# Squared norms of q by a product with a column of ones, in place of transposes with squares along the rows (Gated DeltaNet and Mamba-2 trunk, one core)

## The chip, the core and the metric

The program runs on one core of a Trainium2 chip. A core has a matrix engine (TensorE; PE in the profile, and PEld for its weight loads), a vector engine (VectorE, DVE), an activation engine (ScalarE, ACT), a general engine (GpSimd, POOL) and SyncE (SP), which here issues nearly all transfers. Each engine runs its own list of instructions in order and waits on semaphores for the others. Matrix products and transposes write to PSUM, everything else lies in SBUF or in device memory. The metric is device microseconds of one execution; lower is better.

## What is computed

Two layers over a sequence of 1024 tokens, all in float32. The first is a gated DeltaNet with 8 query/key heads and 16 value heads of width 128; the second, not touched here, is a Mamba-2 mixer. Cut to what matters:

```python
proj = hid @ w_in
qkv = silu(causal_conv(qkv, conv_w))           # 4 taps, per channel
q = _l2norm(q) * 128 ** -0.5                   # _l2norm(x) = x * rsqrt(sum(x*x, -1) + 1e-6)
k = _l2norm(k)
o = _chunk_gated_delta_rule(q, k, v, g, beta)
o = _rmsnorm(o, norm_w) * silu(z)
x = x + o @ w_out
```

The sum of squares of q runs over the 128 channels of a head, one number for each token and head.

## The kernel before

q, k and v are computed transposed: a tile such as `qT` has the 128 channels of a head on the partitions and 512 tokens along the rows, so there are two tiles (`th` 0 and 1) to a head. The normalisation of q is not applied to q itself. The output of a head goes through an RMS norm anyway, so a factor per token can be moved there: `cq` holds, for each token, the epsilon of that norm multiplied by the sum of squares of the token's q. It is read on GpSimd by `so` (L676), just ahead of the power of -0.5 (L678).

The first layer runs over 8 groups (one q/k head and two value heads each). For each group:

- `q_halves`, two `v_halves` and `k_halves` project 512 tokens at a time. One half is 24 products of 128x512 in `ps_proj` (L165 to L167: weights and activations are split into a high and a low part, three products for each of 8 input blocks). ACT copies the result to `raw` (L197) and scales it to `acc` (L200), DVE adds three taps (L204), ACT takes a tanh `th` (L184) and DVE multiplies (L185); for q that gives `qT`.
- What has to be done with a finished half, for q the function `stats`, is put on a list `later` and issued behind the products of the next half, so that TensorE does not stand at it.
- `k_products` squares k for the triangular system and fills `nte` (L437, L441, L451), with decays `lt` from ACT (L418).
- `inverse` inverts the triangular blocks. It stores parts of `nte` to device memory (`xd`, L470), loads them back in another layout (`X`, L473), sets a diagonal on GpSimd (L474), and then runs 31 pairs of DVE instructions, `tm` (L485) and `Dt` (L487).
- `scan` walks over 8 chunks of 128 tokens with a state `S`: a product of k with S (L626), `vpp` on DVE (L629), a product with the inverse (L634), `p` on ACT (L637), a product for the new state (L643), `S` on DVE (L646, L649). Beside it run the output (L661, L663, `o`, `yn`) and the gate `z` (products L227 to L229). `store` transposes `yn` (L66) into `ps_tr`.

The work of neighbouring groups overlaps, and its order on each engine is made by the compiler's list scheduler, which takes instructions by priority and by the readiness that its own model of time gives. A small edit in one function can therefore move instructions of others. Only the order of DVE in the preparation of the first group is written by hand.

`ps_pt` is a ring of two PSUM banks, shared by `stats`, the transposes of v, `k_products` and `inverse`. The tag `th` is a ring of two SBUF tiles, so far for the tanh alone.

In the profile a float32 product appears as two records of weight load and matmul each, a transpose or a product of the split operands as one.

Of the kernel before, what the change touches and what calls it, by code (L numbers as in the profile page):

```python
# [8 lines left out]
F32 = mybir.dt.float32  # L9
F32R = mybir.dt.float32r  # L10
AF = mybir.ActivationFunctionType
ALU = mybir.AluOpType
# [3 lines left out]
EPS = 1e-6  # L16
P = 128
# [7 lines left out]
def hybrid_trunk(  # L25
# [6 lines left out]
    nc = tc.nc  # L32
    x, out = x[0], out[0]
# [6 lines left out]
    cv = ctx.enter_context(tc.tile_pool(name="cv", bufs=2))  # L40
# [12 lines left out]
    ident = const.tile([P, P], F32, tag="ident", name="ident")  # L53
    make_identity(nc, ident)
    ones = const.tile([P, P], F32, tag="ones", name="ones")
# [9 lines left out]
    def turn_pe(dst, src, eye):  # L65
        nc.tensor.transpose(dst, src, eye)  # L66
# [115 lines left out]
    def silu2(dst, src):  # L182
        th = cv.tile([P, 512], F32, tag="th", name="th")
        nc.scalar.activation(th, src, AF.Tanh, scale=0.5)  # L184
        nc.vector.scalar_tensor_tensor(out=dst, in0=th, scalar=1.0, in1=src, op0=ALU.add, op1=ALU.mult)  # L185

    def conv_halves(w_in, col0, hid, cw, ti, bias, emit):
        raws = []

        def consume(th, pt):  # L190
            raw = cv.tile([P, 515], F32, tag="raw", name="raw", bufs=3)
            raws.append(raw)
            if th == 0:
                nc.gpsimd.memset(raw[:, 0:3], 0.0)
            else:
                nc.gpsimd.tensor_copy(raw[:, 0:3], raws[0][:, 512:515])
            nc.scalar.copy(raw[:, 3:515], pt)  # L197
            acc = cv.tile([P, 512], F32, tag="acc", name="acc", bufs=3)
            if bias is None:
                nc.scalar.activation(acc, pt, AF.Copy, scale=cw[:, 96 + ti:97 + ti])  # L200
            else:
                nc.scalar.activation(acc, pt, AF.Identity, scale=cw[:, 96 + ti:97 + ti], bias=bias)  # L202
            for k in range(3):
                nc.vector.scalar_tensor_tensor(out=acc, in0=raw[:, k:k + 512],  # L204
                                               scalar=cw[:, k * 32 + ti:k * 32 + ti + 1], in1=acc,
                                               op0=ALU.mult, op1=ALU.add)
            emit(th, acc)

        yield from proj_halves(w_in, col0, hid, consume)
# [193 lines left out]
    with tc.tile_pool(name="gw", bufs=2) as gw:  # L403
# [140 lines left out]
        def q_halves(g):  # L544
            qT = GS[g]["qT"] = [gw.tile([P, 512], F32, tag="qT", name="qT", bufs=3) for _ in range(2)]
            cq = GS[g]["cq"] = st.tile([P, NT], F32, tag="cq", name="cq")

            def emit(th, acc):
                silu2(qT[th], acc)
                later.append(lambda: stats(th))  # L550

            def stats(th):
                pt = ps_pt()
                for j in range(4):
                    turn_pe(pt[:, j * P:(j + 1) * P], qT[th][:, j * P:(j + 1) * P], ident)
                for j in range(4):
                    nc.scalar.activation(pt[:, j * P:(j + 1) * P], pt[:, j * P:(j + 1) * P], AF.Square,
                                         accum_out=cq[:, th * 4 + j:th * 4 + j + 1])
                if th == 1:
                    nc.gpsimd.tensor_scalar(out=cq, in0=cq, scalar1=4.0 * EPS, scalar2=EPS * P,  # L560
                                            op0=ALU.add, op1=ALU.mult)

            yield from conv_halves(gw_in, g * P, hid, cw_gdn, g, None, emit)

# [429 lines left out]
```

## Time and profile before

| | |
|---|---|
| median of 3 runs | 1995.43 us (1994.64 to 2000.03) |
| the profiled execution | 1990.66 us, its span 1989.0 us |
| TensorE busy | 1919.1 us (96% of the span), weight loads 1639.7 us (82%) |
| VectorE, ScalarE, GpSimd busy | 1305.7 us (66%), 1063.4 us (53%), 411.6 us (21%) |

The span is the time from the first to the last instruction; 1.7 us of the profiled execution lie outside it. The first layer's groups run from about 100 us to about 900 us. A busy TensorE is not one at its peak: its matmuls are pipelined, so records overlap, and the time that a product costs is read from start to start.

### The profile page before, as it was taken

Reading aid. Unit: us, or ns where it says so; the run is one execution under the profiler, and the core shown is the slowest. Engines: PE = TensorE matmul, PEld = TensorE weight load, DVE = VectorE, ACT = ScalarE, POOL = GpSimd, SP = SyncE. Lnnn points to the kernel's source line nnn. Section 1 sums busy time; section 2 is a strip of 40 time slices with the busy share of each in tenths; the row PEclk is TensorE's granted clock in tenths of the full one; section 3 lists DMA queues with packets and bytes.
Section 4 is the critical chain, followed back from the end, with each engine's and each line's share of the span. In section 5 each row is a group of like instructions: output and inputs, shape, how many; then the busy total and the mean of one; then the engine's idle time right before and its main releaser. Section 6 shows DMA issues by size and latency. Waiting matters only on the chain.

```text
span 1989.0 us, 36043 instructions
## 1 busy us (share of the span) xinstructions
PE 1919.1 (96%) x12974; PEld 1639.7 (82%) x12974; DVE 1305.7 (66%) x2915; ACT 1063.4 (53%) x2893; POOL 411.6 (21%) x818
## 2 busy tenths in 40 slices
PE   7997999999999999999999999999999999999998
PEld 5786888888888888897778788888888888888886
DVE  6797685778677776844354676657666676767333
ACT  5635656575656666564343554544555555555332
POOL 1101211212122212100000032423333243332000
PEclk9997999999999999999999999999999999999999
DMA  4421323232232323235574232222222223236654
GB/s 141 117 54 49 98 56 84 67 78 75 57 93 52 99 49 105 58 94 157 152 221 133 64 91 80 69 84 80 64 80 57 80 75 83 78 104 195 203 170 142
DMA packets 284789, 193.35 MB, mean 97 GB/s; under 512 B 65425, under 2 KB 246338, under 8 KB 284610
## 3 DMA queue, kind: packets, MB, share of 16 engines
q1 hardware_dynamic: 284610, 191.05, 34.2%
q8 instruction: 102, 1.67, 0.4%
q14 instruction: 77, 0.63, 0.1%
HBM read 159.34 MB, written 31.65 MB: 96 GB/s over the span
## 4 chain that ended last, share of the span: by engine, by line
PE 75%; DMA 9%; DVE 7%; ACT 4%; POOL 2%; issue 2%; SPq 1%; POOLq 0%; DVEq 0%; ACTq 0%
PE ps_proj L165 9%; PE ps_proj L166 9%; PE ps_proj L167 9%; PE ps_proj L347 6%; PE ps_proj L349 6%; PE ps_proj L348 5%; PE ps_proj L227 5%; PE ps_proj L228 4%; PE ps_proj L229 4%; DMA gcrow<-gcr_s 2%; PE ps_tr L66 2%; PE ps_pt L66 2%; DMA X<-xd 2%; DVE acc L204 2%; PE ps_sc L895 1%
## 5 line engine op out<-in xcount | busy, mean ns | idle before, releaser
L165 PE MATMUL ps_proj<-hid_h,wh 128*128 128x512 f32 x1024 | 412.9, 403 | 3.4 <-ACT acc L200 3.2
L167 PE MATMUL ps_proj<-hid_h,wl 128*128 128x512 f32 x1024 | 404.9, 395 | 0.0
L166 PE MATMUL ps_proj<-hid_l,wh 128*128 128x512 f32 x1024 | 403.6, 394 | 0.0
L227 PE MATMUL ps_proj<-zh,hid_h 128*128 128x256 f32 x1024 | 300.5, 293 | 1.0 <-DVE z L234 1.0
L229 PE MATMUL ps_proj<-zh,hid_l 128*128 128x256 f32 x1024 | 295.4, 288 | 0.0
L228 PE MATMUL ps_proj<-zl,hid_h 128*128 128x256 f32 x1024 | 295.4, 288 | 0.0
L165 PEld LDWEIGHTS ps_proj<-hid_h,wh 128*128 128x128 f32 x1024 | 192.7, 188 | 43.9 <-ACT acc L200 4.0
L167 PEld LDWEIGHTS ps_proj<-hid_h,wl 128*128 128x128 f32 x1024 | 192.5, 188 | 40.3
L166 PEld LDWEIGHTS ps_proj<-hid_l,wh 128*128 128x128 f32 x1024 | 192.9, 188 | 35.4
L347 PE MATMUL ps_proj<-woh,yh 128*128 128x512 f32 x512 | 205.2, 402 | 4.6 <-ACT yh L86 3.2
L348 PE MATMUL ps_proj<-wol,yh 128*128 128x512 f32 x512 | 204.4, 400 | 0.8 <-DVE wol L87 0.7
L349 PE MATMUL ps_proj<-woh,yl 128*128 128x512 f32 x512 | 203.1, 399 | 0.8 <-DVE yl L87 0.7
L227 PEld LDWEIGHTS ps_proj<-zh,hid_h 128*128 128x128 f32 x1024 | 196.3, 192 | 6.0 <-DVE z L234 2.3
L228 PEld LDWEIGHTS ps_proj<-zl,hid_h 128*128 128x128 f32 x1024 | 196.4, 192 | 3.0
L229 PEld LDWEIGHTS ps_proj<-zh,hid_l 128*128 128x128 f32 x1024 | 196.4, 192 | 0.3
L204 DVE SCALAR_TENSOR_TENSOR acc<-raw,cw_ssd,acc 128x512 f32<-128x512 f32 x192 | 156.5, 815 | 45.2 <-ACT acc L202 42.5
L86 ACT CAST yh<-yr 128x512 fp32r<-128x512 f32 x128 | 79.1, 619 | 142.2 <-PE ps_proj L348 90.8
L87 DVE TENSOR_TENSOR yl<-yr,yh 128x512 fp32r<-128x512 f32 x128 | 89.0, 696 | 98.7 <-ACT yh L86 98.3
L204 DVE SCALAR_TENSOR_TENSOR acc<-raw,cw_gdn,acc 128x512 f32<-128x512 f32 x192 | 145.9, 761 | 11.8 <-ACT acc L200 10.2
L87 DVE TENSOR_TENSOR wl<-wr,wh 128x512 fp32r<-128x512 f32 x128 | 89.3, 698 | 68.3 <-ACT wh L86 67.7
L317 POOL TENSOR_SCALAR_AFFINE_SELECT gcrow<-gcrow 128x512 f32<-128x512 f32 x128 | 92.1, 722 | 197.1 <-DMA gcrow<-gcr_g 141.8
L676 POOL TENSOR_SCALAR so<-so,cq 128x2 f32<-128x2 f32 x64 | 27.3, 426 | 462.7 <-ACT yn L675 462.7
(240 smaller groups left out, 3872.0 us busy)
## 6 DMA issues: line engine op xcount, KB each, us to landing
wr<-in_gdn_w_in_dram SPq DMA_DIRECT2D x96, 256.0 KB, 3.0
wr<-in_ssd_w_in_dram SPq DMA_DIRECT2D x96, 256.0 KB, 2.9
gcrow<-gcr_g SPq DMA_DIRECT2D x64, 256.0 KB, 3.6
yr<-y0d SPq DMA_DIRECT2D x64, 256.0 KB, 3.4
gcrow<-gcr_s SPq DMA_DIRECT2D x64, 256.0 KB, 3.9
yr<-y1d SPq DMA_DIRECT2D x64, 256.0 KB, 3.2
y0d<-yg SPq DMA_DIRECT2D x64, 128.0 KB, 1.9
wr<-in_gdn_w_out_dram SPq DMA_DIRECT2D x32, 256.0 KB, 3.5
```

The lines of the kernel that those rows point to most:

```text
L87: nc.vector.tensor_tensor(out=lo, in0=src, in1=hi.bitcast(F32), op=ALU.subtract)
L165: nc.tensor.matmul(pt[0:nco], hi[:, j, 0:nco], xh[:, j, :], start=first, stop=False)
L166: nc.tensor.matmul(pt[0:nco], hi[:, j, 0:nco], xl[:, j, :], start=False, stop=False)
L167: nc.tensor.matmul(pt[0:nco], lo[:, j, 0:nco], xh[:, j, :], start=False, stop=last)
L204: nc.vector.scalar_tensor_tensor(out=acc, in0=raw[:, k:k + 512], scalar=cw[:, k * 32 + ti:k * 32 + ti + 1], in1=acc, op0=ALU.mult, op1=ALU ...
L227: nc.tensor.matmul(pt, xh, zh[:, k, :], start=k == 0, stop=False)
L228: nc.tensor.matmul(pt, xh, zl[:, k, :], start=False, stop=False)
L229: nc.tensor.matmul(pt, xl, zh[:, k, :], start=False, stop=k == KT - 1)
L317: nc.gpsimd.affine_select(out=t, in_=t, pattern=[[0, 4], [1, P]], compare_op=ALU.is_ge, fill=-1e30, base=0, channel_multiplier=-1)
L347: nc.tensor.matmul(pt, yh[:, j, :], hi[:, j, :], start=first, stop=False)
L348: nc.tensor.matmul(pt, yh[:, j, :], lo[:, j, :], start=False, stop=False)
L349: nc.tensor.matmul(pt, yl[:, j, :], hi[:, j, :], start=False, stop=last)
```

## The change

For each of the 16 halves of q, four transposes into PSUM and four squares along the rows (ACT, each with its accumulator read) are replaced by one square of the whole 128x512 tile on ACT into an SBUF tile of the ring `th`, and four products of a squared 128x128 block, as the stationary operand, with one column of ones. The sums then lie in four columns of a PSUM tile. The scaling with epsilon moves from GpSimd, once a group for 8 columns, to DVE, once a half for 4 columns, and reads PSUM.

```diff
             def stats(th):
+                sq = cv.tile([P, 512], F32, tag="th", name="sq")
+                nc.scalar.activation(sq, qT[th], AF.Square)
                 pt = ps_pt()
                 for j in range(4):
-                    turn_pe(pt[:, j * P:(j + 1) * P], qT[th][:, j * P:(j + 1) * P], ident)
-                for j in range(4):
-                    nc.scalar.activation(pt[:, j * P:(j + 1) * P], pt[:, j * P:(j + 1) * P], AF.Square,
-                                         accum_out=cq[:, th * 4 + j:th * 4 + j + 1])
-                if th == 1:
-                    nc.gpsimd.tensor_scalar(out=cq, in0=cq, scalar1=4.0 * EPS, scalar2=EPS * P,
-                                            op0=ALU.add, op1=ALU.mult)
+                    nc.tensor.matmul(pt[:, j:j + 1], sq[:, j * P:(j + 1) * P], ones[:, 0:1], start=True, stop=True)
+                nc.vector.tensor_scalar(out=cq[:, th * 4:th * 4 + 4], in0=pt[:, 0:4], scalar1=4.0 * EPS,
+                                        scalar2=EPS * P, op0=ALU.add, op1=ALU.mult)
```

Lines behind the edit have numbers smaller by 2 in the changed kernel: L626 becomes L624, L634 becomes L632, L646 and L649 become L644 and L647.

The scheduler puts the new instructions where its model has them ready, and the order of the rest of the first layer moves with them; in the second layer the order is that of before. Two places in a group matter to the prediction, and one of them is shown on two engines.

**The second half of q, on TensorE**, in a group where the first scan steps are under way (402 us in the profile of before). Before, the last scan product is followed by the transposes of `qT`:

```order
L643 MATMUL ps_sc<-p,ktok 128x128 x2
L661 MATMUL ps_sc<-S,qT 128x256
L663 MATMUL ps_sc<-p,att 128x128 x2
L626 MATMUL ps_sc<-S,kT 128x256
L66 MATMUL ps_pt<-ident,qT 128x128 x4
L66 MATMUL ps_pt<-ident,acc 128x128 x4
L165 MATMUL ps_proj<-hid_h_96,wh 128x512
```

Now the same place of the changed kernel:

```order
L641 MATMUL ps_sc<-p,ktok 128x128 x2
L659 MATMUL ps_sc<-S,qT 128x256
L661 MATMUL ps_sc<-p,att 128x128 x2
L624 MATMUL ps_sc<-S,kT 128x256
L557 MATMUL ps_pt<-ones,sq 128x1 x4
L632 MATMUL ps_sc<-vpp,nte 128x128 x2
L165 MATMUL ps_proj<-hid_h_96,wh 128x512
```

The new products stand where the transposes stood, directly behind the product of k with S, and now need the square `sq` from ACT where the transposes needed `qT` from DVE. The transposes of `acc` (of v) have moved further back.

**The same place on ACT.** Before, `L670` (the output's scaling) is followed by the eviction `L200`, and the squares read PSUM behind it:

```order
L637 ACTIVATE p<-ps_sc,bp 128x128 x2
L233 ACTIVATE tz<-ps_proj 128x256
L670 ACTIVATE o<-ps_sc,eg_g 128x128 x2
L200 ACTIVATE acc<-ps_proj,cw_gdn 128x512
L557 ACTIVATE ps_pt,cq<-ps_pt 128x128 x2
L578 ACTIVATE vs<-ps_pt,skh 128x128 x4
```

In the changed kernel:

```order
L635 ACTIVATE p<-ps_sc,bp 128x128 x2
L233 ACTIVATE tz<-ps_proj 128x256
L668 ACTIVATE o<-ps_sc,eg_g 128x128 x2
L554 ACTIVATE sq<-qT 128x512
L184 ACTIVATE th<-acc 128x512
L200 ACTIVATE acc<-ps_proj,cw_gdn 128x512
```

The square of the whole tile stands in front of the eviction.

**The border between two groups, on DVE.** Here `k_products` of one group ends, the scan of the next begins (`S` copied by L646), and the inverse of the group behind it waits for `X` at its first `tm`. Before, the borders alternate between two orders. One of them (466 us in the profile of before):

```order
L451 SCALAR_TENSOR_TENSOR nte<-ps_pt,nbp,lt 128x128 x4
L204 SCALAR_TENSOR_TENSOR acc<-raw,cw_gdn,acc 128x512
L646 COPY S<-ps_sc 128x256
L615 TENSOR_TENSOR att<-ps_tr,lt 128x256
L204 SCALAR_TENSOR_TENSOR acc<-raw,cw_gdn,acc 128x512 x2
L615 TENSOR_TENSOR att<-ps_tr,lt 128x256
L234 SCALAR_TENSOR_TENSOR z<-tz,ps_proj 128x256
L185 SCALAR_TENSOR_TENSOR qT<-th,acc 128x512
L629 SCALAR_TENSOR_TENSOR vpp<-ps_sc,negc_g,vs 128x128 x2
L87 TENSOR_TENSOR wl<-wr,wh 128x512
L485 TENSOR_TENSOR tm<-Dt,X 128x2
```

The same border in the changed kernel:

```order
L451 SCALAR_TENSOR_TENSOR nte<-ps_pt,nbp,lt 128x128 x3
L627 SCALAR_TENSOR_TENSOR vpp<-ps_sc,negc_g,vs 128x128 x2
L613 TENSOR_TENSOR att<-ps_tr,lt 128x256
L185 SCALAR_TENSOR_TENSOR qT<-th,acc 128x512
L87 TENSOR_TENSOR wl<-wr,wh 128x512 x2
L204 SCALAR_TENSOR_TENSOR acc<-raw,cw_gdn,acc 128x512 x2
L558 TENSOR_SCALAR cq<-ps_pt 128x4
L204 SCALAR_TENSOR_TENSOR acc<-raw,cw_gdn,acc 128x512
L485 TENSOR_TENSOR tm<-Dt,X 128x2
```

The copy of `S` (L644) stands eight rows ahead of these. So the last writes of `nte` (L451), from which `X` is made, now come behind that copy and directly ahead of `vpp`, and three taps (L204), with the new `cq` (L558) among them, stand between and the first `tm`. Three of the six borders of before stand like that already (369, 579 and 790 us), three like the piece above (257, 468 and 678 us); in the changed kernel all six have the new order.

## Rows read from the trace of the kernel before

**Rows 1.** The page: busy time of each engine, and the chain that ended last.

```profile
PE 1919.1 (96%) x12974; PEld 1639.7 (82%) x12974; DVE 1305.7 (66%) x2915; ACT 1063.4 (53%) x2893; POOL 411.6 (21%) x818
PE 75%; DMA 9%; DVE 7%; ACT 4%; POOL 2%; issue 2%; SPq 1%; POOLq 0%; DVEq 0%; ACTq 0%
```

**Rows 2.** Busy time by stretch: PE, PEld, DVE, ACT, POOL, clock, DMA.

```profile
150.00:190.00 40.00, 29.11 (x269) 23.96 (x268) 27.24 (x94) 21.99 (x74) 6.30 (x14) 0.74 0.22 56
190.00:900.00 710.00, 685.88 (x5521) 607.00 (x5520) 519.58 (x1395) 439.26 (x1350) 132.25 (x255) 0.99 0.30 76
```

**Rows 3.** What stats costs, by form, 0 to 1050 us: busy, mean ns.

```profile
L557 ACT ACTIVATE ps_pt<-ps_pt 128x128 f32<-128x128 f32 x64 | 17.3, 271 | 1.9 <-PE ps_pt L66 1.1
L557 ACT ACTIVATION_READ_ACCUMULATOR ps_pt<-ps_pt 128x1 f32 x64 | 12.6, 197 | 0.0
L560 POOL TENSOR_SCALAR cq<-cq 128x8 f32<-128x8 f32 x8 | 2.0, 256 | 5.2 <-ACT ps_pt L557 4.7
```

**Rows 4.** Near relatives of the new instructions, by form: busy, mean ns.

```profile
L107 ACT ACTIVATE xn<-xrow 128x512 f32<-128x512 f32 x5 | 3.2, 638 | 3.3 <-DMA xrow<-x1d 3.3
L443 DVE TENSOR_SCALAR sk<-sk 128x4 f32<-128x4 f32 x16 | 2.6, 165 | 0.1
```

**Rows 5.** Timeline of PE and PEld around transposes of q: start, duration.

```profile
79.46 0.39 PE L166 MATMUL ps_proj<-hid_l,wh 128*128 128x512 f32 x1
79.69 0.60 PE L66 MATMUL ps_pt<-ident,qT 128*128 128x128 f32 x4
80.04 0.48 PE L167 MATMUL ps_proj<-hid_h,wl 128*128 128x512 f32 x1
80.36 0.40 PE L165 MATMUL ps_proj<-hid_h,wh 128*128 128x512 f32 x1
...
80.01 0.19 PEld L167 LDWEIGHTS ps_proj<-hid_h,wl 128*128 128x128 f32 x1
80.12 0.19 PEld L165 LDWEIGHTS ps_proj<-hid_h,wh 128*128 128x128 f32 x1
```

**Rows 6.** The chain in order of time: start, length, records.

```profile
46.91 0.89 PE ps_pt L437 x8
...
222.66 2.00 PE ps_pt L521 x32
```

**Rows 7.** Timeline of PE and DVE at a border of the one kind.

```profile
369.19 0.70 PE L626 MATMUL ps_sc<-S,kT 128*128 128x256 f32 x2 [1.23 <-DVE S L649]
371.82 0.33 PE L66 MATMUL ps_tr<-ident,yn 128*128 128x128 f32 x1 [1.93 <-DVE yn L680]
...
367.81 0.16 DVE L485 TENSOR_TENSOR tm<-Dt,X 128x2 f32<-128x2 f32 x1 [5.31 <-POOL X L474]
...
368.80 0.34 DVE L649 SCALAR_TENSOR_TENSOR S<-S,egl_g,ps_sc 128x128 f32<-128x128 f32 x1
```

**Rows 8.** Busy time by stretch around that border.

```profile
366.00:372.00 6.00, 2.84 (x13) 1.79 (x12) 3.47 (x19) 3.58 (x12) 1.34 (x5) 1.00 0.27 52
372.00:376.00 4.00, 4.00 (x22) 3.94 (x22) 3.90 (x16) 1.68 (x5) 0.00 (x0) 0.57 0.11 33
```

**Rows 9.** A border of the other kind: stretches, then PE and DVE.

```profile
255.00:261.00 6.00, 4.94 (x36) 4.43 (x35) 5.07 (x19) 3.36 (x10) 1.22 (x3) 1.00 0.44 134
261.00:267.00 6.00, 5.26 (x27) 4.03 (x25) 5.28 (x22) 4.51 (x18) 1.89 (x5) 1.00 0.05 15
...
266.32 0.33 PE L66 MATMUL ps_tr<-ident,yn 128*128 128x128 f32 x1 [0.74 <-DVE yn L680]
...
255.63 0.16 DVE L485 TENSOR_TENSOR tm<-Dt,X 128x2 f32<-128x2 f32 x1 [3.73 <-POOL X L474]
```

**Rows 10.** The second half of q: timeline of PE, DVE and ACT.

```profile
402.82 0.66 PE L66 MATMUL ps_pt<-ident,qT 128*128 128x128 f32 x4 [0.39 <-DVE qT L185]
...
402.08 0.68 DVE L185 SCALAR_TENSOR_TENSOR qT<-th,acc 128x512 f32<-128x512 f32 x1
...
401.95 0.63 ACT L670 ACTIVATE o<-ps_sc,eg_g 128x128 f32<-128x128 f32 x2 [0.94 <-PE ps_sc L663]
```

## The prediction, made before the changed kernel was run

> **What bounds the kernel now.** I read the page first, then busy time by stretch, then the groups of instructions of `stats`, and last the timeline at the places where the order changes. The page [rows 1] gives TensorE 1919.1 us of work in a span of 1989.0, and the chain that ended last is 75% TensorE: the bound is one engine's throughput, and nothing else is over 82%. In the stretch of the full groups, 190 to 900 us [rows 2], TensorE is busy 685.88 of 710 us at a granted clock of 0.99 (2.4 GHz), so it idles 24.1 us; DVE works 519.58 us (73%), ACT 439.26 us (62%). What the change takes from ACT or POOL can shorten the kernel only through those 24.1 us; what it does to TensorE's own list shows in full. So three questions decide: do the new products cost TensorE more or less than the transposes; what do they wait for; and what happens at the group borders, where the order moves.
>
> **The work, engine by engine.** On ACT the change removes 64 squares (17.3 us) and 64 accumulator reads (12.6 us) [rows 3], 29.9 us. It adds 16 squares of 128x512; the nearest row is a square of that shape, 638 ns [rows 4], so 10.2 us: ACT is relieved of 19.7 us. POOL loses 8 instructions, 2.0 us [rows 3]. DVE gains 16 `tensor_scalar` of 128x4, by the like-shaped row 165 ns each [rows 4], 2.6 us. I cost all three at nothing: TensorE's 96% hides them. Should DVE's cover fail, it is those 2.6 us; what ACT's relief could give back at most is a rival below. The epsilon step moving off POOL adds no transfer and passes no queue, and `so`, its reader, comes a whole projection later.
>
> **Term 1, TensorE's own time.** A transpose of `qT` is one record. A projection product takes 0.23 us from start to start and stays at that when nothing intervenes. Around four transposes [rows 5] the starts are 79.46 (L166), 79.69 (first transpose), 80.04 (L167), 80.36 (L165): from 79.46 to 80.36 is 0.90 us, of which two products account for 2 × 0.23 = 0.46. Four transposes therefore cost 0.44 us, 0.11 each. The new product has a squared 128x128 block as its weights and a single column to stream. As a float32 product it is two records, so a half has 8 loads of 128x128 f32. What such a load costs when little is streamed is seen twice. In [rows 5] the loads for L167 and L165 start 0.11 us apart (80.01, 80.12), although the product between them streams longer than that, so a load is never seen to be free. And the 8 records of the k squares, f32 128x128 [rows 6], take 0.89 us, 0.111 each, where by columns they should stream in a quarter of a 512-column product, 0.23 / 4 = 0.06. Loads pace them, and a product of one column has the same loads. I take 8 × 0.111 = 0.89 us a half against 0.44, **+0.45 us, ×16 halves = +7.2 us**. Bounds: if one column cost nothing at all, −0.44 × 16 = −7.0 us; if the cost per record were that of the 64x64 records of `inverse`, 2.00 / 32 = 0.0625 us [rows 6], 8 × 0.0625 = 0.50, +0.06 × 16 = +1.0 us. I stay at the upper end because the k squares have the same 128x128 weights, and the 64x64 records only half the columns. The page TensorE: Matmul & The Clock Gate of the Trainium skill, section LDWEIGHTS (loading the stationary operand), has the load time as columns over 1.2, about 107 ns for 128 columns; by that, an estimate, term 1 would be +6.7 us. The spacing in these rows agrees with it.
>
> **Term 2, the wait for the square.** For first halves of q other work stands around `stats`, and `sq` is ready behind the next half's products. For second halves, in the groups in which a scan runs, the order on TensorE puts the products directly behind the product of k with S, where the transposes of `qT` stood. There the transposes already wait 0.39 us for `qT` [rows 10]: L185 starts at 402.08 and lasts 0.68, so `qT` is done at 402.76 and they start at 402.82. The new products need `sq`, which ACT can start only after 402.76 (L670 ends at 401.95 + 0.63 = 402.58, so ACT is free) and which takes 0.64 us: they start at about 403.45, 0.64 us later. Behind them stand L632, for which the scan waits, and the next projection; nothing ready may pass. The order shows this place in six groups: 6 × 0.64 = **+3.8 us**. Lower bound 0, if L632 has to wait for `vpp` until then anyway. Upper bound 5, if the eviction L200, now behind the square on ACT, comes late as well and a projection bank is freed 0.2 us later each time.
>
> **Term 3, the borders.** Before, the six borders alternate between two orders. At 369 us (the order which all six now have) TensorE waits 1.23 us for `S` of L649 and 1.93 us for `yn` [rows 7]; it is busy 2.84 of 6 us, and from 372 the clock falls to 0.57 for 4 us [rows 8]. About 3.4 us at the lower level (1.2 GHz) in place of 2.4 lose 1.7 us of work. Together 1.23 + 1.93 + 1.7 = 4.9 us. A border of the other kind [rows 9] idles 1.06 of the 6 us (busy 4.94) and then 0.74 us for `yn`, 1.8 us in all, with the clock at 1.00. If the three cheap borders became like the dear ones, the cost would be 3 × (4.9 − 1.8) = 9.3 us. But the dear border is not dear by its order alone: there the first `tm` waits 5.31 us for `X` [rows 7] against 3.73 us [rows 9], and in the new order three taps and `cq` now stand ahead of `tm`, so DVE has something to do meanwhile. Lower bound 0; I take a third, **+3.1 us**, since the new row order is like the dear kind in where `S` stands, but not in what waits.
>
> **Sum.** 7.2 + 3.8 + 3.1 = 14.1 us. On the profiled execution of 1990.66 us that makes 2004.8; the median of the three runs, 1995.43, is 4.77 us above that execution, and the timed median of the changed kernel should be so too: 2009.5 us. About 0.3%, 6 us, is what a measurement here can tell from no change (the three runs of before lie 5.4 us apart).
>
> **Rivals.**
>
> *The products are cheap, and the rest evens out.* Term 1 lies between −7.0 and +1.0 us, with a middle of −3.0; terms 2 and 3 at 3.8 and 0 to 3.1 bring the sum to about +1.5, 1997 us, within 0.3%. For it: two loads for one column could overlap each other as no row here shows. Against it: the 0.111 of the k squares. The same page of the Trainium skill, section Back-to-back issue gap, gives a floor of about 25 ns for matmuls of 1 to 64 columns. By that estimate 8 records would be 0.2 us a half and term 1 −3.8 us; the same section also says that in a stream of loads and matmuls both set the spacing, and the k squares bear out the latter.
>
> *The borders go the dear way in full, and more.* All three at 9.3 in place of 3.1 makes +20.3, or 2015.7 us; if the longer stall at the second halves also drops the clock at six places as it does at 372 us, 1.7 each, +10.2, or 2026 us. For it: the order is that of the dear border, and a 1.23 and a 1.93 us wait there preceded the drop. Against it: a stall of about a microsecond alone did not drop it at 255 us (1.06 us of idle, clock 1.00 [rows 9]).
>
> *Faster, by ACT's relief.* 19.7 us less work on ACT, on which evictions, `p`, `o` and `th` queue, brings TensorE's inputs sooner and shrinks its 24.1 us of idle time. Terms 1 and 2 stay at 11.0 us; if all 19.7 came back, 11.0 − 19.7 = −8.7, or 1986.7 us. It decides as soon as over 17 us (11 + 6) of the idle time go. Against it: ACT is busy only 62% there, and the longest waits of the borders are for `S`, `yn` and `X`, whose last steps run on DVE and POOL [rows 7].
>
> **How the numbers follow.** The forecast has a chance of 0.56, with a range of its own from 2002 (term 1 and nothing else, 1995.43 + 7.2) to 2016. Cheap products 0.18, borders in full 0.18, ACT's relief 0.08. Slower: 0.56 + 0.18 = 0.74; same 0.18; faster 0.08. The range goes from 1996, just under the centre of the cheap case, to 2021, the middle of the dear case between 2015.7 and 2026; outside lie the fast case, a little of the cheap one and half of the dear one, together about 0.2.
>
> **What would show it.** Term 1: the four products of a half as 8 records over 0.89 us, their loads 0.11 us apart; wrong if they come much closer. Term 2: a wait of TensorE for ACT's `sq` of about 1 us (0.39 + 0.64) at six second halves; wrong if L632 would have waited as long. Term 3: idle time and clock drops at 257, 468 and 678 us, which now look like those at 369; wrong if these clocks stay at 1.00 or if the other three get better. The busy time of ACT should fall by 20 us. The forecast as a whole is wrong if TensorE's idle time between 190 and 900 us falls well under 24.1 us, or if its records there take less than before.

## Result, and the profile after

The changed kernel takes 2014.62 us (median of 5 runs, 2007.74 to 2018.02) against 1995.43 us, a ratio of 1.0085 with a 95% interval from 1.0063 to 1.0107: 17 us more, 13 to 21. The forecast was 2009.5 us, 14.1 us more. The profiled execution below is the fastest of the five, 2007.74 us.

The page of the changed kernel: span, busy time of each engine, and the chain that ended last.

```profile
span 2005.9 us, 36087 instructions
PE 1927.0 (96%) x13038; PEld 1645.8 (82%) x13038; DVE 1308.2 (65%) x2931; ACT 1051.7 (52%) x2781; POOL 417.6 (21%) x810
PE 70%; DMA 11%; DVE 8%; ACT 4%; issue 3%; POOL 3%; SPq 1%; POOLq 0%; DVEq 0%; ACTq 0%
```

Against [rows 1] the span is 16.9 us longer, while TensorE is busy only 7.9 us more: TensorE's share of the chain fell from 75% to 70%, and DMA and DVE gained 3 points together. A part of the loss is work, the larger part is waiting. ACT is 11.7 us less busy and not 20: the 17.3 and 12.6 us of [rows 3] add up records that overlap in time, a square and its accumulator read, and together the two kept ACT busy for 24.4 us and not 29.9. The kernel is slower all the same.

Its new products, by line (duration in ns: least, median, most).

```profile
L557 PE MATMUL ps_pt<-ones,sq x128: 164/250/352, 79.4 to 845.0; 128*128 128x1 f32 x128
```

The 64 products are 128 records, two to each. The square (L554, 631 ns) and the scaling (L558, 155 ns) cost what their relatives in [rows 4] did.

Its timeline at three places: a first half where nothing is waited for, a second half of q, and a border (start, duration, in brackets the idle time before it and what ended it).

```profile
79.19 0.39 PE L166 MATMUL ps_proj<-hid_l,wh 128*128 128x512 f32 x1
79.42 0.95 PE L557 MATMUL ps_pt<-ones,sq 128*128 128x1 f32 x8
80.23 0.48 PE L167 MATMUL ps_proj<-hid_h,wl 128*128 128x512 f32 x1
...
406.76 0.68 PE L624 MATMUL ps_sc<-S,kT 128*128 128x256 f32 x2
408.29 0.60 DVE L627 SCALAR_TENSOR_TENSOR vpp<-ps_sc,negc_g,vs 128x128 f32<-128x128 f32 x2
408.53 1.05 PE L557 MATMUL ps_pt<-ones,sq 128*128 128x1 f32 x8 [1.09 <-ACT sq L554]
409.45 0.69 PE L632 MATMUL ps_sc<-vpp,nte 128*128 128x128 f32 x4
...
264.58 0.16 DVE L485 TENSOR_TENSOR tm<-Dt,X 128x2 f32<-128x2 f32 x1 [5.19 <-POOL X L474]
266.04 0.60 DVE L647 SCALAR_TENSOR_TENSOR S<-S,egl_g,ps_sc 128x128 f32<-128x128 f32 x2
266.69 0.70 PE L624 MATMUL ps_sc<-S,kT 128*128 128x256 f32 x2 [1.60 <-DVE S L647]
269.40 0.33 PE L66 MATMUL ps_tr<-ident,yn 128*128 128x128 f32 x1 [2.01 <-DVE yn L678]
```

First place: from L166 to L167 it is 80.23 − 79.19 = 1.04 us. With four transposes in between it was 80.04 − 79.46 = 0.58 [rows 5], so a half costs 0.46 us more. Second: TensorE stands 1.09 us for `sq`, where before it stood 0.39 us for `qT` [rows 10]. Third: `tm` waits 5.19 us for `X`, the copy of `S` stands behind it in DVE's list, TensorE waits 1.60 us for that `S` and 2.01 us more for `yn`. This border is the 257 us one of before, which idled 1.06 and 0.74 us [rows 9].

Busy time in the stretch behind that border (columns as in [rows 2]).

```profile
270.00:275.00 5.00, 5.00 (x30) 4.88 (x29) 4.79 (x17) 1.68 (x5) 0.00 (x0) 0.66 0.09 26
```

Here the clock now falls as it did at 372 us before [rows 8]: the 0.34 missing over 5 us are 1.7 us of work.

What TensorE waited for from 190 to 900 us, in sum, times and longest: first the kernel before.

```profile
PE ps_tr L66 <- DVE yn L680: 7.5, 6, 1.9
PE ps_sc L626 <- DVE S L649: 2.8, 3, 1.2
PE ps_proj L165 <- ACT acc L200: 3.2, 3, 1.2
PE ps_pt L66 <- DVE qT L185: 1.2, 3, 0.4
DVE tm L485 <- POOL X L474: 26.4, 6, 5.3
```

And the changed kernel.

```profile
PE ps_tr L66 <- DVE yn L678: 11.7, 6, 2.0
PE ps_sc L624 <- DVE S L647: 8.0, 6, 2.0
PE ps_pt L557 <- ACT sq L554: 5.8, 6, 1.1
DVE tm L485 <- POOL X L474: 26.1, 6, 5.2
```

The last line is the one to read first: DVE waits for `X` as long as before, 26 us at six borders. What changed is who stands behind it: TensorE now waits for `S` at five borders and not at three (and a sixth time, 0.52 us, at 857 us, ahead of the last group's scan). At the border of 482 us it waits for `yn` alone, 1.76 us. One kind of wait went: L165 waited 3.2 us for the eviction `acc` at the three borders of the other kind, at 258, 469 and 679 us, and at none now.

### The profile page after: what moved, and what is told of

Its sections match the earlier page's. It is cut to its first block, busy times and chain, and to the rows that moved or that the text cites. A ratio compares the mean times of both kernels' runs of the same rounds, so it can differ in the third digit from the quotient of the medians.

```text
span 2005.9 us, 36087 instructions
## 1 busy us (share of the span) xinstructions
PE 1927.0 (96%) x13038; PEld 1645.8 (82%) x13038; DVE 1308.2 (65%) x2931; ACT 1051.7 (52%) x2781; POOL 417.6 (21%) x810
## 4 chain that ended last, share of the span: by engine, by line
PE 70%; DMA 11%; DVE 8%; ACT 4%; issue 3%; POOL 3%; SPq 1%; POOLq 0%; DVEq 0%; ACTq 0%
PE ps_proj L165 9%; PE ps_proj L166 8%; PE ps_proj L167 8%; PE ps_proj L227 5%; PE ps_proj L347 5%; PE ps_proj L349 5%; PE ps_proj L228 5%; PE ps_proj L348 5%; PE ps_proj L229 5%; DMA X<-xd 2%; PE ps_tr L66 2%; DMA gcrow<-gcr_s 2%; DVE acc L204 2%; PE ps_pt L66 1%; PE ps_sc L893 1%
## 5 line engine op out<-in xcount | busy, mean ns | idle before, releaser
L165 PE MATMUL ps_proj<-hid_h,wh 128*128 128x512 f32 x1024 | 412.3, 403 | 0.0
L167 PE MATMUL ps_proj<-hid_h,wl 128*128 128x512 f32 x1024 | 406.8, 397 | 0.0
L166 PE MATMUL ps_proj<-hid_l,wh 128*128 128x512 f32 x1024 | 404.1, 395 | 0.0
L167 PEld LDWEIGHTS ps_proj<-hid_h,wl 128*128 128x128 f32 x1024 | 193.0, 188 | 40.5
L165 PEld LDWEIGHTS ps_proj<-hid_h,wh 128*128 128x128 f32 x1024 | 192.8, 188 | 39.9 <-DVE z L234 0.4
L166 PEld LDWEIGHTS ps_proj<-hid_l,wh 128*128 128x128 f32 x1024 | 193.2, 189 | 35.6
L204 DVE SCALAR_TENSOR_TENSOR acc<-raw,cw_ssd,acc 128x512 f32<-128x512 f32 x192 | 155.8, 812 | 45.4 <-ACT acc L202 42.6
L204 DVE SCALAR_TENSOR_TENSOR acc<-raw,cw_gdn,acc 128x512 f32<-128x512 f32 x192 | 146.6, 764 | 17.8 <-ACT acc L200 16.2
L674 POOL TENSOR_SCALAR so<-so,cq 128x2 f32<-128x2 f32 x64 | 31.5, 492 | 509.4 <-ACT yn L673 509.4
L317 POOL TENSOR_SCALAR_AFFINE_SELECT gcrow<-gcrow 128x512 f32<-128x512 f32 x128 | 96.9, 761 | 161.8 <-DMA gcrow<-gcr_g 104.7
```

What stands on the lines that cost most here:

```text
L165: nc.tensor.matmul(pt[0:nco], hi[:, j, 0:nco], xh[:, j, :], start=first, stop=False)
L166: nc.tensor.matmul(pt[0:nco], hi[:, j, 0:nco], xl[:, j, :], start=False, stop=False)
L167: nc.tensor.matmul(pt[0:nco], lo[:, j, 0:nco], xh[:, j, :], start=False, stop=last)
L317: nc.gpsimd.affine_select(out=t, in_=t, pattern=[[0, 4], [1, P]], compare_op=ALU.is_ge, fill=-1e30, base=0, channel_multiplier=-1)
```

## The experiments

Each was timed beside the kernel before on the same chip, but not all on one chip; so the ratios, which are to the kernel before, are what to compare.

### The scaling on DVE alone

```diff
-                if th == 1:
-                    nc.gpsimd.tensor_scalar(out=cq, in0=cq, ...)
+                nc.vector.tensor_scalar(out=cq[:, th * 4:th * 4 + 4], in0=cq[:, th * 4:th * 4 + 4], ...)
```

> One part of the change alone, on the kernel before: transposes, squares along the rows and accumulator reads stay; only the scaling with epsilon moves from GpSimd (8 instructions of 8 columns) to DVE (16 of 4 columns, out of SBUF). My theory, by which the cost lies in the products, in their wait for sq and at the borders, expects no change: 1995 us, within 3, with TensorE's idle time still about 54 us. The rival, that 16 small instructions in DVE's queue are what delays S and yn at the borders, expects 2 to 17 us more, with more idle time at the six borders.

Measured: 2007.02 us, ratio 1.0056 (1.0035 to 1.0077). My expectation failed. The borders keep the order of before, with `cq` added to DVE's list. Waits of DVE and TensorE in 190 to 900 us, and DVE's timeline at one border:

```profile
DVE cq L559 <- ACT ps_pt L557: 12.9, 5, 4.0
PE ps_tr L66 <- DVE yn L679: 12.2, 7, 2.1
...
264.58 0.17 DVE L559 TENSOR_SCALAR cq<-cq 128x4 f32<-128x4 f32 x1 [1.62 <-ACT ps_pt L557]
265.52 0.60 DVE L648 SCALAR_TENSOR_TENSOR S<-S,egl_g,ps_sc 128x128 f32<-128x128 f32 x2
```

Sixteen instructions of 0.17 us cost far more than themselves, because they wait in DVE's list for ACT's last accumulator, and `S` and `yn` stand behind them. In the changed kernel the same instruction reads the products' PSUM tile, and no wait of DVE before L558 is shown. So this part costs about 11 us beside the old squares, but it doesn't follow that it costs anything beside the new ones; the run without it, below, answers that in part.

### One record to a product

```diff
-                sq = cv.tile([P, 512], F32, tag="th", name="sq")
+                sq = cv.tile([P, 512], F32R, tag="th", name="sq")
-                    nc.tensor.matmul(pt[:, j:j + 1], sq[...], ones[:, 0:1], ...)
+                    nc.tensor.matmul(pt[:, 2 * j:2 * j + 2], sq[...], ones_r, ...)
```

> The changed kernel with sq and the ones in the type of the split operands (float32r), so that a product is one record in place of two (two columns of ones, since one is not to be had in that type; the squares are rounded to that type). If records of a 128x128 weight block cost 0.111 us each, a half's products take 4 x 0.111 = 0.44 us from start to start, in place of 0.89, as much as the transposes did: 16 x 0.45 = 7.2 us less than the changed kernel, about 2007 us, and within 4 of that since the borders may be ordered otherwise; the six waits for sq stay, 0.7 to 1.1 us each. The rival, that the number of records is hidden and only the order counts, expects 2014 us where the borders stall as in the changed kernel, and no change of TensorE's time without its idle time and its slow clock.

Measured: 2008.65 us, ratio 1.0065 (1.0046 to 1.0085), 4 us under the changed kernel by the ratios. The records behave as forecast (shown below, in the run that adds the other border), but the borders fell otherwise. At one of them TensorE waited 5.23 us, the longest wait for `S` in any run. Its timeline:

```profile
373.08 0.16 DVE L487 TENSOR_TENSOR tm<-Dt,X 128x2 f32<-128x2 f32 x1 [7.96 <-POOL X L476]
375.27 1.22 PE L626 MATMUL ps_sc<-S,kT 128*128 128x256 f32 x2 [5.23 <-DVE S L649]
```

Here `tm` stood longer for `X`, and TensorE longer for the `S` behind it, than at any border of the changed kernel. The two don't go in step from border to border, though: in the changed kernel 4.91 us of `tm` went with 0.69 us for `S` (at 375 us), 4.33 us with 2.02 (at 592 us). By its total this run neither supports nor refutes the price of a record.

### Each product twice

```diff
-                for j in range(4):
+                for j in (0, 1, 2, 3, 0, 1, 2, 3):
```

> The changed kernel with each of the four products of a half issued twice, into the same columns. At 0.111 us a record 8 more records cost 0.89 us a half, 14.2 us over 16 halves, also at the borders and the second halves: about 2029 us, within 4 for borders that are ordered otherwise. If a record of one column cost what the floor of short products would suggest (under 0.03 us), it would be less than 4 us more: 2018 us at most.

Measured: 2031.61 us, ratio 1.0173 (1.0151 to 1.0195), 17 us over the changed kernel. TensorE's timeline at the first half:

```profile
78.59 0.39 PE L166 MATMUL ps_proj<-hid_l,wh 128*128 128x512 f32 x1
78.82 1.84 PE L557 MATMUL ps_pt<-ones,sq 128*128 128x1 f32 x16
80.53 0.48 PE L167 MATMUL ps_proj<-hid_h,wl 128*128 128x512 f32 x1
```

From L166 to L167 it is 1.94 us in place of 1.04: 8 more records cost 0.90, or 0.112 each, and 16 halves 14.4 of the 17 us. Cheap short products are refuted.

### `S` ahead of `tm`

```diff
-            nc.gpsimd.memset(X.rearrange("p s c -> p (s c)")[:, 0:1024:33], 1.0)
+            if g > 1:
+                yield
+                nc.gpsimd.tensor_scalar(out=X.rearrange(...)[:, 0:1024:33], in0=GS[g - 1]["S"][:, 0:32],
+                                        scalar1=0.0, scalar2=1.0, op0=ALU.mult, op1=ALU.add)
+            else: ...                     # the memset as before
...
-                if s in (20, 14, 9, 4):
+                if s in (20, 14, 9, 4) and (s < 20 or g < 2):
                     yield
...
-                    S = chain(n, S)
+                    S = E["S"] = chain(n, S)
```

> The changed kernel with another order at the borders: the diagonal of X is set by a GpSimd instruction that reads the second state S of the scan (times zero plus one) and so comes behind it, and the first tm with it; the inverse's first steps are issued one slot later. In the changed kernel the second copy of S (L647) stands on DVE behind a tm that waits about 5 us for X; now S stands ahead of tm. My theory of the borders (DVE stands at tm, S and yn behind it, TensorE behind these) expects the 1.6 us waits for S and the 2.0 us waits for yn to go at the six borders, and the drops of the clock behind them: 19.9 us of idle time plus about 4 x 1.7 us are there now; half to two thirds of that should come back, so 1996 to 2004 us. The rival, that TensorE waits there for the inverse's own results or for DMA, expects no gain, 2014 us or more, since tm comes later.

Measured: 1986.1 us, ratio 0.9951 (0.9932 to 0.9971): 27 us less than the changed kernel by the ratios, more than expected, and less than the kernel before. TensorE's wait for `yn` in 190 to 900 us, and the timeline of DVE at the first border:

```profile
PE ps_tr L66 <- DVE yn L683: 3.7, 5, 1.2
...
263.43 0.61 DVE L652 SCALAR_TENSOR_TENSOR S<-S,egl_g,ps_sc 128x128 f32<-128x128 f32 x2 [2.75 <-PE ps_sc L646]
266.54 0.20 DVE L490 TENSOR_TENSOR tm<-Dt,X 128x2 f32<-128x2 f32 x1 [2.17 <-POOL X L476]
```

`S` comes as soon as its product is done, 3 us ahead of `tm`, and the wait for it, 8.0 us in the changed kernel, is gone from the list; the one for `yn` fell from 11.7 to 3.7. Together that is 16 us. From 200 to 800 us the granted clock is 1.00, and none of the drops of the changed kernel there (at 271, 411, 595 and 704 us) is left: 4 × 1.7 = 7 us. Others come later in the program, so that over the two profiled executions the mean clock rises only from 0.986 to 0.987, 2 us; their spans differ by 2005.9 − 1986.6 = 19.3 us. Over all timed runs the mean clock rises from 0.983 to 0.988, by my estimate 9 us, and with the 16 that is 25 of the 27. That `tm` comes later costs nothing that shows. The edit also moves the points at which the inverse gives way to other work, so it is not the place of `S` alone that changed.

### Both: one record, and `S` ahead of `tm`

> The kernel of the run before (S ahead of tm at the borders) with products of one record each, as in the run with float32r squares (the squares are rounded to that type). Here the borders no longer stall, so the price of the records stands alone: 16 x 0.45 = 7.2 us less than 1986, that is 1979 us, within 3; the waits for sq at the six second halves stay (0.6 to 1.1 us each). The rival, that the records' price was hidden and the run with one record gained by its other borders, expects 1984 to 1988 us.

Measured: 1971.37 us, ratio 0.9884 (0.9865 to 0.9904), the fastest of all: 22 us less than the kernel before, 13 less than with two records by the ratios. Its timeline at a half where nothing is waited for and at a second half, and what TensorE waits for:

```profile
357.51 0.58 PE L564 MATMUL ps_pt<-ones_r,sq 128*128 128x2 f32 x4
357.96 0.37 PE L231 MATMUL ps_proj<-zh,hid_l 128*128 128x256 f32 x1
...
395.56 0.70 PE L631 MATMUL ps_sc<-S,kT 128*128 128x256 f32 x2
397.55 0.71 PE L639 MATMUL ps_sc<-vpp,nte 128*128 128x128 f32 x4
...
PE ps_pt L564 <- ACT sq L561: 4.3, 6, 1.1
PE ps_sc L639 <- DVE vpp L634: 4.3, 6, 0.8
```

Four records over 357.96 − 357.51 = 0.45 us; 0.45 × 16 = 7.2 us is the expected part. The gain is larger than the expectation allowed for (1979 us, within 3). Over all timed runs the mean granted clock is 0.990 against 0.988 with two records, by my estimate 4 us of the rest; the intervals of the two ratios, 4 us either way each, cover what is left. Why the clock stands better here the runs don't show.

### The products one half later

```diff
                 nc.scalar.activation(sq, qT[th], AF.Square)
+                later.append(lambda: sums(th, sq))
+
+            def sums(th, sq):
                 pt = ps_pt()
```

> As the run with one record and S ahead of tm, and the products are issued one half later than the square, which lies in a tile of its own (one buffer): sq is then long done when TensorE comes to the products. My theory expects the waits for sq at the six second halves to go (0.56 to 1.09 us each, 4.8 us in the run with S ahead of tm): 4 to 5 us less than that kernel, about 1974 us. The rival, that the scan's next product would have waited there for vpp anyway, expects the same idle time in front of L632's product in place of sq's, and no gain (1979 us).

Measured: 1974.45 us, ratio 0.9900 (0.9880 to 0.9919). The scheduler put the products where they had been, directly behind the product of k with S, and `sq` is waited for six times as before, 4.6 us in all; so the run tells nothing of what that wait costs. What did change is who follows them, as the timeline of TensorE at one second half shows:

```profile
397.91 0.68 PE L634 MATMUL ps_sc<-S,kT 128*128 128x256 f32 x2
399.31 0.61 PE L567 MATMUL ps_pt<-ones_r,sq 128*128 128x2 f32 x4 [0.72 <-ACT sq L561]
399.77 0.66 PE L68 MATMUL ps_pt<-ident,acc 128*128 128x128 f32 x4
```

The transposes of `acc` stand there, as they did before the change, and not the product that needs `vpp`. The time is no better for it (0.9884 without).

### The kernel before, with `S` ahead of `tm`

The same edit of the borders as above, in the kernel before.

> The kernel before the change with S ahead of tm at the borders (the same GpSimd instruction that reads S). If this order is worth at the borders of before what they lose now (13.5 us of idle time at six borders and three drops of the clock, 1.7 us each), 12 to 19 us come back: 1977 to 1984 us, and the change itself then costs terms 1 and 2 alone, 10 to 12 us against 1986. The rival, that only borders in the order of the changed kernel stall, expects three of the six to gain: about 1986 to 1990 us.

Measured: 1999.81 us, ratio 1.0028 (1.0015 to 1.0040). Both expectations failed. TensorE's longest waits in 190 to 900 us, and one of them in the timeline:

```profile
PE ps_proj L227 <- ACT acc L200: 11.2, 4, 6.1
PE ps_tr L66 <- DVE yn L685: 2.4, 3, 1.5
...
578.26 1.31 POOL L317 TENSOR_SCALAR_AFFINE_SELECT gcrow<-gcrow 128x512 f32<-128x512 f32 x2 [6.36 <-DMA gcrow<-gcr_g]
578.92 0.40 ACT L418 ACTIVATE lt<-gcrow,neggc_g 128x128 f32<-128x128 f32 x1 [6.28 <-POOL gcrow L317]
581.69 0.58 PE L227 MATMUL ps_proj<-zh,hid_h 128*128 128x256 f32 x1 [4.27 <-ACT acc L200]
```

The waits for `yn` fell from 7.5 to 2.4 us and those for `S` from 2.8 to 0.3, so the edit does its work here too. But in the new order ACT stands 6.28 us at `lt`, whose `gcrow` comes by DMA, with an eviction behind it that frees TensorE's bank. It is the same pattern on another engine. What the change costs with quiet borders on both sides is therefore not measured.

### The scaling off DVE

```diff
-                nc.vector.tensor_scalar(out=cq[:, th * 4:th * 4 + 4], in0=pt[:, 0:4], ...)
+                nc.scalar.copy(cq[:, th * 4:th * 4 + 4], pt[:, 0:4])
+                if th == 1:
+                    nc.gpsimd.tensor_scalar(out=cq, in0=cq, ...)
```

> The changed kernel with the scaling taken off DVE: ACT copies the four columns out of PSUM, and GpSimd scales once a group as before. The last writes of nte still come behind the first copy of S at the borders, so my theory (it is that order that makes tm wait 5 us for X and S wait behind it) expects what the changed kernel has, 2014 us within 5, with waits for S or yn of 1.5 to 2 us at the six borders. The rival, that cq in DVE's queue makes the borders dear, as the run that moved it alone may suggest, expects 2000 to 2006 us.

Measured: 2012.35 us, ratio 1.0087 (1.0067 to 1.0106), the ratio of the changed kernel. Three of TensorE's waits in 190 to 900 us:

```profile
PE ps_sc L626 <- DVE S L649: 10.0, 6, 3.1
PE ps_sc L643 <- ACT p L637: 6.2, 4, 3.0
PE ps_tr L66 <- DVE yn L680: 2.7, 4, 2.1
```

Six waits for `S` without `cq` on DVE: it isn't `cq` that makes TensorE wait for `S` in the changed kernel, and that part of the rival falls. The total says less than it seems to. The waits for `yn` fell from 11.7 to 2.7 us, and waits for `p` came in their place, where ACT stands for `lt` and its `gcrow` (3.10 us at 591 us); so whether `cq` has a part in the waits for `yn` this run leaves open.

### Each square twice

```diff
-                nc.scalar.activation(sq, qT[th], AF.Square)
+                for _ in range(2):
+                    nc.scalar.activation(sq, qT[th], AF.Square)
```

> The kernel with one record and S ahead of tm (1971 us), with each square of q on ACT done twice into the same tile: 16 squares, 10 us, more on ACT. By the compiler's model the products are then ready later, and it places them behind two projection products of the next half in place of directly behind the product of k with S; nobody's result changes. If the wait for sq at the six second halves costs what it shows (4.3 us in that kernel), it goes and the time falls by 2 to 4 us, to 1967 to 1969, in spite of the 10 us more on ACT. The rival, that the scan's next product would wait for vpp at that place as long (so the wait for sq costs nothing), expects 1971 us or, if ACT's work counts, up to 1981.

Measured: 1973.22 us, ratio 0.9877 (0.9850 to 0.9904), no other than the kernel it started from (0.9884). The wait for `sq` is gone, and its place is taken, as the rival said: `vpp` is now waited for 12 times and not 6. TensorE's only wait of weight in 190 to 900 us, and one of its places:

```profile
PE ps_sc L640 <- DVE vpp L635: 12.0, 12, 1.3
...
393.95 0.70 PE L632 MATMUL ps_sc<-S,kT 128*128 128x256 f32 x2
395.94 0.71 PE L640 MATMUL ps_sc<-vpp,nte 128*128 128x128 f32 x4 [1.29 <-DVE vpp L635]
```

From the product of k with S to the one that needs `vpp` it is 395.94 − 393.95 = 1.99 us, as long as with the products and their wait in between (397.55 − 395.56). The 10 us more on ACT cost nothing measurable either.

### The square in four blocks

```diff
-                nc.scalar.activation(sq, qT[th], AF.Square)
+                for j in range(4):
+                    nc.scalar.activation(sq[:, j * P:(j + 1) * P], qT[th][:, j * P:(j + 1) * P], AF.Square)
```

> The same kernel with the square of q in four instructions of 128x128 in place of one of 128x512: the first product needs the first block alone, 0.27 us after qT in place of 0.64, while ACT has about 7 us more to do in all. The products stay directly behind the product of k with S. If the wait for sq is on the path, its 0.56 to 1.06 us become about 0.4 us shorter at each of six places, 2 us in all, 1969 us; the rival expects the same time, 1971 us, with the wait moved to L632's product or into the later blocks.

Measured: 1974.74 us, ratio 0.9893 (0.9871 to 0.9915), again no gain. The waits for `sq` are halved, from 4.3 to 2.0 us, and the time doesn't follow.

## Why the prediction held, step by step

**TensorE's own time, 7.2 us forecast.** It is 0.46 us a half, 7.4 us in 16. Twice the products cost 0.112 us for each further record, and products of one record took 0.45 us a half, what the transposes took. The Trainium skill, page TensorE: Matmul & The Clock Gate, section LDWEIGHTS (loading the stationary operand), has the load time as columns over 1.2, by estimate 107 ns for 128 columns; the 0.111 to 0.112 us of these rows agree within 5%, and the floor of 25 ns in its section Back-to-back issue gap, which by estimate would make 8 records 0.2 us, is not what a row here shows.

**The wait for the square, 3.8 us forecast.** TensorE's idle time at these places grew by 5.8 − 1.2 = 4.6 us, so size and place were right. Behind one of the six places the clock dropped as well (at 411 us), 1.7 us that only the dear rival had allowed for. Whether the wait for `sq` is the cause is only half settled. In the kernel with one record, take the wait away (each square twice) or shorten it (four blocks), and nothing comes back: L640 then waits 1.29 us for `vpp`. There, what I gave as the reason for the lower bound, that the scan's next product would have to wait anyway, is what happens. The changed kernel is another case, since its products take twice as long. In the timeline of the result `vpp` is done at 408.29 + 0.60 = 408.89 us and L632 starts at 409.45, 0.56 us later; at the six places it is 0.38 to 0.57 us, where with one record it is 0.05 us at five of them. So some 2.7 us of the wait should have been on the path there, an estimate; no run took the wait out of the changed kernel itself. In the order of before, the transposes of `acc` and projection products stand behind the transposes of `qT`, ahead of the product that needs `vpp`; in the new order nothing does. With one record to a product that alone isn't what costs: the run with the products one half later has the transposes of `acc` there again, and neither the wait for `sq` nor the time fell. Work ahead of the new products, which could fill the wait, no run has.

**The borders, 3.1 us forecast.** Here the size failed. I took a third of 9.3, since `tm` at the cheap borders waited 3.73 us for `X` and not 5.31, and DVE had taps to do ahead of it. But the waits for `S` and `yn` grew by (8.0 − 2.8) + (11.7 − 7.5) = 9.4 us. In the forecast's own terms, idle time and clock together, the three cheap borders cost (1.06 + 0.74) + (1.22 + 0.41) + (0.89 + 0.60) = 4.9 us before, of which 3.2 were waits for `acc` that have gone, and cost (1.60 + 2.01 + 1.7) + 1.76 + (1.68 + 1.99 + 1.7) = 12.4 us now: 7.5 us more, near the upper bound of 9.3. Two of the three became dear in full; the one at 482 us did not, and its clock stayed at 1.00. The other three cost 13.7 us before and 13.6 after: at 375 us a drop of the clock went, at the other two the waits for `S` grew. A clock that stays up at one of the cheap three, and a dear one that gets better, are both what I had named as signs against this term. The shorter wait of `tm` was no sign of a cheaper border: over six borders it is 26 us in both kernels, and what counts is what stands behind `tm`. The run with `S` ahead of `tm` shows it.

**What came back, which I did not see.** Ahead of the last group's scan TensorE was idle 2.6 of 10 us at a clock of 0.66 before, and is not now. First the kernel before, then the changed one:

```profile
840.00:850.00 10.00, 7.40 (x123) 6.33 (x121) 6.21 (x14) 6.18 (x14) 2.14 (x4) 0.66 0.60 187
```

```profile
856.00:868.00 12.00, 11.38 (x196) 10.42 (x189) 8.49 (x21) 7.82 (x22) 4.23 (x4) 1.00 0.48 143
```

That is 2.6 + 3.4 us before against 0.6, a gain of 5.4; what brought it no run isolates. With it the sum is 7.4 + 4.6 + 1.7 + 7.5 − 5.4 = 15.8 us, of the 16.9 by which the spans differ; the other 1.1 I can't assign. That the forecast's total came out near is in part luck: a border term that was too small met a gain that was left out.

**The rivals.** Cheap products are refuted. (Their sum, given as about +1.5, runs by its own terms from 0.8 to 3.9, with a middle of 2.4; this changes no verdict.) ACT's relief did not come back: it was smaller than the 19.7 us I took, since those added up overlapping records, the idle time grew, and in the run with each square twice 10 us more on ACT changed nothing. The dear borders came for the greater part, 7.5 of 9.3 us, and of the clock drops at six second halves which that rival added, one came.

## What to carry to other kernels

In this kernel a product with one column of ones is no cheap reduction: its price goes by the records, here 0.111 to 0.112 us for each 128x128 block of weights with one column or two, so count records, and halve them where the precision of the sum allows it. When an edit shuffles a scheduler's order, look at each engine's list for an instruction that waits for a transfer, and at what stands behind it: putting the state's update ahead of one such wait at the borders gave back more (27 us) than the whole change had cost (17 us), and the same edit in the kernel before the change only moved the stall to another engine. A wait that the trace names is not yet a cost; take it away and see whether the next one takes its place.

## What the runs showed that I had not expected

Sixteen instructions of 0.17 us on DVE, some with a late input, cost about 11 us over the program (ratio 1.0056), by what stood behind them and by the clock after that (0.984 in the profiled execution, against 0.987 before). And of the changed kernel's borders not every stall was followed by a drop of TensorE's clock: 1.60 and 2.01 us at 265 us were, 0.69 and 2.02 us at 374 us were not, and at 411 us a drop came behind a second half that had waited 1.09 us.
